# An encoder kernel on one Trainium2 core: the convolution half of the output projection, issued pair by pair of token tiles, and GpSimd's low parts held in program order

## The chip, the core and the metric

One Trainium2 chip, of which the program uses one core. The metric is the device time of one launch in microseconds (us); lower is better. The engines are called PE (matrix products), DVE (vector), ACT (scalar), POOL (GpSimd) and SP (the queue from which the DMAs of this kernel are issued). Each engine works through its own queue in order; semaphores make one wait for another.

## The reference

A prompt and a sample of 512 tokens each, with 16 meta tokens in front, go through one layer in float32. What matters here, cut:

```
z = rms(h) @ w_in                        # -> c_val, c_gate, cq, ckv, k_rope
u = silu(layernorm(conv(c_val * sigmoid(c_gate))))      # 512 channels per token
o = attention(cq, ckv, k_rope)                          # 512 channels per token
h = h + concat([u, o]) @ w_out                          # 1024 x 1024
hf = rms(h)
h = h + (silu(hf @ w_gate) * (hf @ w_up)) @ w_down      # 1024 -> 2816 -> 1024
y = rms(h)
```

## The kernel before

Products are made from pairs: a float32 operand is split into a high part (ACT's cast) and a low part (the rest, a subtraction on DVE or POOL), and `mm3` adds high x high, high x low and low x high, three matmuls for each 128 rows of the contraction.

The 1024 real tokens are eight tiles of 128, `t` = 0 to 7; tile `t` and tile `t + 4` (prompt and sample) form **pair** `t`. The residual rows of tile t are in `hres[t]` (in the rows `h` for 0 to 2, `slots` for 3 to 7).

**Output projection.** `w_out_block(half, dq, t)` adds to quarter `dq` (256 columns) of `hres[t]` the product of one half of the 1024 channels: 12 matmuls of 256 columns into one of four PSUM banks `pt` (L992, the helper's L167 in the rows), then one addition on DVE (L994). Half 1 (attention) comes first, for all tiles. Half 0 (convolution) is 32 blocks, (dq, t); its four weight tiles are `wo[0]`, `wo[2]`, `wo[4]`, `wo[6]`, and they are in the four buffers that the first gate matrix's operands (`wc`) take over, quarter by quarter.

**From a finished tile to the feed-forward's operands.** The feed-forward's products are Strassen products of 2 x 2 blocks (seven products instead of eight; a Winograd form), in which the two token halves (tiles 0 to 3 and 4 to 7) and the two channel halves are the blocks. For each pair t:

- `sq(t)`: once all four quarters of tile t are in, SP stores `hres[t]`, ACT squares and sums it (L192), POOL makes the reciprocal root from it (L193, L194).
- `sc(t)`: DVE scales the tile, two instructions of 512 columns with both tensors in SBUF (L1045).
- `tu(t, s)`: PE transposes tile t (s = 0) or tile t + 4 (s = 1) in 8 matmuls (L1060) into one of two PSUM tiles `px`.
- `do(t, stages)`: the high parts on ACT (L1064, and the copies L1077 and L1080), the sums `t1` to `t4` on DVE (L1086, L1087, L1091, L1094) and the low parts (L1067). Low parts of `a11`, `a12`, `a22` are made by DVE from PSUM; those of the sums `s2`, `s3` (stage x) and `s1`, `s4` (stage y) by POOL, or by DVE where `S_DVE[t]` lists 0, 1 (x) or 2, 3 (y). In the rows `s3` and `a11`, `a22` are called `act`.

**Feed-forward units.** A unit is 256 columns of `w_gate` or `w_up`. `co(j)` (`Unit.comb`) makes the j-th weight operand of unit 0: sums of the loaded blocks on DVE (L1136), the high part on ACT (L1152), the low part on POOL (L1154). `pr(j)` makes product j of unit 0 for the first 256 of a half's 512 token columns, that is for the pairs 0 and 1; the loop over units makes the other 256 columns of unit 0 (pairs 2 and 3) and after each of these products calls `comb(j)` of unit 1. Unit 1's weights are loaded into `hres[2]` and `hres[6]`, which are free once pair 2's low parts are made. From unit 1 on a product has 512 columns.

**What sets the order.** A scheduler orders the instructions of each engine by priorities and a modelled time; those that went through `pin` while `pinned[0]` is set keep the order of the program. It is set from the list of steps on to the end of unit 0. The list is written out by hand:

```
def run(steps):
    for step in steps:
        if isinstance(step, tuple):
            w_out_block(0, *step)
        else:
            step()
```

Of the kernel before, what the change touches and what calls it, by code (L numbers as in the profile page):

```python
# [12 lines left out]
F32 = mybir.dt.float32  # L13
# [71 lines left out]
LO_W = 1024  # L85
ORDER = "Q K S0 S1 T0 T3 M0 T1 M1 S2 T2 M2 T4 M4 M3 S3 E C"
U0_DVE = ()
S_DVE = ((), (), (), (0, 1))


def real_col(s):
# [10 lines left out]
def encoder_kernel(ctx: ExitStack, tc: tile.TileContext, x, meta, gains, w_in, w_kr, small, conv_w, wq, wk, wv,  # L102
# [10 lines left out]
    def name(p):  # L113
        n_tile[0] += 1
        return f"{p}_{n_tile[0]}"
# [9 lines left out]
    def pin(ins):  # L125

        return in_order(ins) if pinned[0] else ins

    def in_order(ins):
        tc.keep_in_program_order(ins)  # L130
        return ins
# [3 lines left out]
    def slot(i):  # L135
        return slots[:, i, :]
# [399 lines left out]
    sq = [slot(0), slot(1)]  # L536
# [451 lines left out]
    def w_out_block(half, dq, t):  # L988
        s, cs, ds = t // 4, slice(t % 4 * 128, t % 4 * 128 + 128), slice(dq * 256, (dq + 1) * 256)
        pt = bank()  # L990
        w = wo[2 * dq + half]
        mm3(pt[:, :256], [(act[half][s][0][:, k, cs], act[half][s][1][:, k, cs]) for k in range(4)],  # L992
            [tuple(wx[:, k * 256:(k + 1) * 256] for wx in w) for k in range(4)])
        pin(nc.vector.tensor_add(hres[t][:, ds], pt[:, :256], hres[t][:, ds]))  # L994
# [27 lines left out]
    a11, a22, s3 = act[0][0], act[1][1], act[0][1]  # L1022
    hf2 = [comb.tile([P, D], F32, name=f"hf{i}") for i in range(2)]
    a12, s1, s2, s4 = (operand(comb, n) for n in ("a12", "s1", "s2", "s4"))


# [9 lines left out]
    def ffn_square(t):  # L1036

        nc.sync.dma_start(h_dram[t * 128:(t + 1) * 128, :], hres[t])
        k4 = hres[t].rearrange("p (k n) -> p k n", k=4)
        ffn_rs[t] = rms_scale(k4, P, s4[1][:, :, 256:512])  # L1040

    def ffn_scale(t):
        for e in range(2):
            h, g = (a[:, e * 512:(e + 1) * 512].rearrange("p (k n) -> p k n", k=4) for a in (hres[t], g_ffn))
            pin(nc.vector.scalar_tensor_tensor(normed_half(t, e), h, ffn_rs[t], g, ALU.mult, ALU.mult))  # L1045

    class Turn:
# [21 lines left out]
        def do(self, stages):  # L1069
            b11, b12 = self.pts[0]  # L1070
            b21, b22 = self.pts[1] if len(self.pts) > 1 else (None, None)
            t1, t2, t3, t4 = self.ts
            own = [nc.vector if i in S_DVE[self.t] else nc.gpsimd for i in range(4)]
            for stage in stages:
                if stage == "a":
                    self.high(a11, b11)
                    pin(nc.scalar.copy(t1, b11))  # L1077
                    self.high(a12, b12)
                elif stage == "A":
                    pin(nc.scalar.copy(t4, b22))  # L1080
                    self.high(a22, b22)
                elif stage == "b":
                    self.low(a11, b11, nc.vector)
                    self.low(a12, b12, nc.vector)
                elif stage == "c":
                    pin(nc.vector.tensor_sub(t3, t1, b21))  # L1086
                    pin(nc.vector.tensor_sub(t1, b22, t3))  # L1087
                    self.high(s2, t1)
                    self.high(s3, t3)
                elif stage == "e":  # L1090
                    pin(nc.vector.tensor_sub(t2, b12, t1))  # L1091
                    self.high(s4, t2)
# [25 lines left out]
    class Unit:  # L1118
# [19 lines left out]
        def comb(self, j):  # L1138
            b11, b12, b21, b22 = (self.block(a, b) for a in range(2) for b in range(2))
            if j == 2:  # L1140
                self.temp("t1", b12, b11)
                self.temp("t2", b22, self.t["t1"])
            if j == 3:
                self.temp("t3", b22, b12)
            if j == 5:
                self.temp("t4", b21, self.t["t2"])
            src = (b11, b21, self.t.get("t2"), self.t.get("t3"), self.t.get("t1"), self.t.get("t4"), b22)[j]
            n = self.u * 7 + j
            if n % 2 == 0:
                two_ops[0] = stream.tile([P, 2, 1024], F32R, tag="pair", bufs=4, name=name("wc"))  # L1150
            w = two_ops[0][:, n % 2, :]
            pin(nc.scalar.copy(w[:, 0:512], src))  # L1152
            lo_eng = nc.vector if self.u in U0_DVE else nc.gpsimd
            lo_eng.tensor_sub(w[:, 512:1024], src, w[:, 0:512].bitcast(F32))  # L1154
# [35 lines left out]
    units = [Unit(u) for u in range(NFF)]  # L1190
# [44 lines left out]
    def w_out_rest(dqs, ts):  # L1235
        for dq in dqs:
            for t in ts:
                w_out_block(0, dq, t)

    w_out_rest(range(3), (0, 4, 1, 5))  # L1240

    pinned[0] = True

# [8 lines that stand above are left out]
    def sq(t):  # L1252
        return lambda: ffn_square(t)

    def sc(t):
        return lambda: ffn_scale(t)

    def co(j):
        return lambda: units[0].comb(j)

    def pr(j):
        return lambda: units[0].product(j, slice(0, 256))
# [3 lines left out]
    def tu(t, s):  # L1266
        def begin():
            if not s:
                turns[t] = Turn(t)
            turns[t].turn(s)  # L1270
        return begin

    def do(t, stages):
        return lambda: turns[t].do(stages)

    units[0].load()
    run([(3, 0), sq(0), (3, 4), sq(4), (3, 1), sq(1), sc(0), (3, 5), sq(5), sc(4), (0, 2), (0, 6),
         tu(0, 0), do(0, "a"), sc(1), (0, 3), tu(0, 1), do(0, "A"), do(0, "b"), (0, 7), do(0, "ce"), sc(5), (1, 2),
         do(0, "xd"), (1, 6), do(0, "y"), (1, 3), co(0), (1, 7),
         tu(1, 0), do(1, "a"), (2, 2), tu(1, 1), do(1, "A"), do(1, "b"), co(1), (2, 6), do(1, "ce"), (3, 2),  # L1280
         do(1, "x"), sq(2), do(1, "d"),
         (3, 6), sq(6), do(1, "y"), co(2), (2, 3), sc(2), (2, 7), sc(6), co(3), co(4), (3, 3), sq(3),
         tu(2, 0), do(2, "a"), tu(2, 1), do(2, "A"), co(5), (3, 7), sq(7)])

    run([pr(0), do(2, "b"), sc(3), co(6), pr(1), do(2, "ce"), pr(2), sc(7), do(2, "x"), pr(3), pr(4),
         tu(3, 0), do(3, "a"), do(2, "dy"), units[1].load, pr(5), do(3, "b"), pr(6), tu(3, 1), do(3, "Ace")])
    left = [[do(3, "x")], [do(3, "dy")]]


    n_pairs = NFF // 2  # L1290
# [3 lines left out]
    def reuse(key):  # L1294
        pool = ops if key.startswith("act") else comb
        return pool.tile([P, 4, SEQ], F32R, tag=key, bufs=1, name=name("re")).rearrange("p a b -> p (a b)")
# [141 lines left out]
    y, junk = (reuse(ld_places[i]).bitcast(F32) for i in (0, 1))  # L1438
# [93 lines left out]
```

## Time and profile before

| | us |
|---|---|
| median of 3 runs | 1107.52 (1107.51 to 1107.55) |
| the profiled execution, its own time | 1107.57 |
| its span, first to last instruction | 1105.8 |
| PE busy in the span | 1081.4 (98%) |
| DVE busy | 824.0 (75%) |
| ACT busy | 498.7 (45%) |
| POOL busy | 477.3 (43%) |

Times in rows are from the span's start; 1.8 us of the profiled execution's time lie around its span. The mean granted clock of PE is 0.992 of full speed. In this program half 0 of the output projection begins at 401.84 us, the products of unit 0 at 458.5, those of unit 1 at 488.43 and those of unit 2 at 508.84. A row of the order in time gives the start, the length, the engine, the line, the operation, what is written and read, and in brackets how long the engine stood idle before it and what released it.

### The profile page before, as it was taken

The page shows a single profiled execution, that of the slowest core. Times are in us where ns is not written, and L with a number is a line of the kernel's source. Part 1 is how long each engine was busy: PE and PEld are TensorE (multiplying, and loading weights), DVE is VectorE, ACT ScalarE, POOL GpSimd, SP SyncE. Part 2 cuts the span into 40 slices and gives each one's busy share as a digit, 9 for nine tenths or more (in the row PEclk, how much of TensorE's full clock was granted, in tenths as well). Part 3 has the DMA queues.
Part 4 walks back from the last instruction along what each step waited for, and adds up shares of the span by engine and source line. Part 5 has one row for each costly group of instructions (what it writes and reads, how often), then busy time and mean ns, then how long its engine had stood idle before and what let it go on. Part 6 is the DMA issues. An engine that isn't in the chain of part 4 may idle for free.

```text
span 1105.8 us, 16021 instructions
## 1 busy us (share of the span) xinstructions
PE 1081.4 (98%) x5922; PEld 935.2 (85%) x5922; DVE 824.0 (75%) x1204; ACT 498.7 (45%) x836; POOL 477.3 (43%) x421
## 2 busy tenths in 40 slices
PE   8999999999999999989999999999999999999997
PEld 8989888888888999878888888888888888888886
DVE  5699997888887546888767776877787595657643
ACT  6554525787786534542333223222323355433331
POOL 4689636563562323865545555554455200000012
PEclk9999999999999999889999999999999999999999
DMA  7211112010111311325264436434542999865503
GB/s 293 78 39 49 39 39 63 37 57 1 39 39 57 116 58 77 127 85 208 94 201 174 145 130 203 159 105 181 190 170 87 306 335 334 284 205 177 181 24 133
DMA packets 71422, 147.08 MB, mean 133 GB/s; under 512 B 6944, under 2 KB 29728, under 8 KB 71344
## 3 DMA queue, kind: packets, MB, share of 16 engines
q1 hardware_dynamic: 71344, 146.06, 38.3%
q8 instruction: 47, 0.77, 0.3%
q14 instruction: 31, 0.25, 0.1%
HBM read 105.92 MB, written 40.11 MB: 132 GB/s over the span
## 4 chain that ended last, share of the span: by engine, by line
PE 83%; DVE 9%; ACT 3%; issue 2%; DMA 2%; POOL 1%; SPq 0%; POOLq 0%; ACTq 0%; DVEq 0%
PE pt L167 59%; PE ps L167 13%; PE pt L797 3%; PE pt L767 2%; PE pt L298 2%; DVE ps L389 2%; DVE ps L397 2%; DVE pacc L399 1%; PE px L277 1%; PE pt L588 1%; ACT p L739 1%; DMA gain<-in_gains_dram 1%; DMA h<-in_w_up_dram 0%; DVE sst L738 0%; DVE kl L156 0%
## 5 line engine op out<-in xcount | busy, mean ns | idle before, releaser
L167 PE MATMUL pt<-act_h,wc 128*128 128x512 f32 (+1 forms) x552 | 177.2, 384 | 0.0
L1154 POOL TENSOR_TENSOR wc<-tt,wc 128x512 fp32r<-128x512 f32 x88 | 123.2, 1416 | 107.8 <-ACT wc L1152 58.4
L167 PEld LDWEIGHTS pt<-act_h,wc 128*128 128x128 f32 x552 | 104.3, 192 | 19.6
L193 POOL TENSOR_SCALAR ms<-ms 128x1 f32<-128x1 f32 x15 | 7.8, 521 | 231.8 <-ACT re L192 213.8
L1152 ACT CAST wc<-tt 128x512 fp32r<-128x512 f32 x88 | 51.6, 619 | 124.5 <-PE pt L167 111.3
L167 PE MATMUL pt<-hn_h,wp 128*128 128x512 f32 (+2 forms) x448 | 107.0, 331 | 0.0
L167 PE MATMUL pt<-act_l,wc 128*128 128x512 f32 (+1 forms) x276 | 105.9, 384 | 0.2 <-DVE act_l L1067 0.2
L1334 DVE TENSOR_TENSOR re<-re,re 128x1024 fp32r<-128x1024 f32 x53 | 64.2, 1224 | 44.8 <-ACT re L1333 43.2
L1333 ACT CAST re<-re 128x1024 fp32r<-128x1024 f32 x53 | 55.3, 1055 | 66.9 <-PE pt L167 22.6
L167 PE MATMUL pt<-re 128*128 128x512 f32 x360 | 84.0, 389 | 0.0
L167 PEld LDWEIGHTS pt<-hn_h,wp 128*128 128x128 f32 x448 | 75.8, 188 | 8.4
L167 PEld LDWEIGHTS pt<-re 128*128 128x128 f32 x360 | 67.6, 188 | 14.0
L152 POOL TENSOR_TENSOR wp<-raw,wp 128x1024 fp32r<-128x1024 f32 x24 | 58.6, 2441 | 40.7 <-ACT wp L149 40.7
L167 PE MATMUL pt<-hn_l,wp 128*128 128x512 f32 (+2 forms) x224 | 74.4, 332 | 0.0
L742 POOL TENSOR_SCALAR p<-p,sst 128x512 f32<-128x512 f32 x64 | 44.2, 696 | 65.0 <-DVE sst L740 57.2
L167 PE MATMUL pt<-wp,act_h 128*128 128x256 f32 x384 | 72.0, 288 | 0.1
L1154 POOL TENSOR_TENSOR wc<-raw,wc 128x512 fp32r<-128x512 f32 x33 | 44.1, 1349 | 52.7 <-ACT wc L1152 52.7
L167 PE MATMUL ps<-re 128*128 128x512 f32 x276 | 63.9, 389 | 0.0
L167 PEld LDWEIGHTS pt<-act_l,wc 128*128 128x128 f32 x276 | 53.0, 192 | 10.1 <-DVE act_l L1067 0.4
L367 POOL TENSOR_TENSOR pacc<-pacc,prod 128x512 f32<-128x512 f32 x43 | 58.3, 1357 | 7.0 <-ACT prod L365 4.3
L167 PEld LDWEIGHTS pt<-wp,act_h 128*128 128x128 f32 x384 | 60.7, 195 | 0.4 <-DVE slots L994 0.4
L167 PEld LDWEIGHTS ps<-re 128*128 128x128 f32 x276 | 51.8, 188 | 10.7
(295 smaller groups left out, 2941.7 us busy)
## 6 DMA issues: line engine op xcount, KB each, us to landing
raw<-in_w_gate_dram SPq DMA_DIRECT2D x22, 512.0 KB, 3.9
hf<-in_w_down_dram SPq DMA_DIRECT2D x44, 256.0 KB, 4.6
re<-in_w_down_dram SPq DMA_DIRECT2D x31, 256.0 KB, 4.6
raw<-in_w_in_dram SPq DMA_DIRECT2D x12, 512.0 KB, 3.6
slots<-in_w_up_dram SPq DMA_DIRECT2D x11, 512.0 KB, 3.5
h<-in_w_up_dram SPq DMA_DIRECT2D x11, 512.0 KB, 5.4
d_t1t<-hf SPq DMA_DIRECT2D x22, 256.0 KB, 5.3
d_t4t<-hf SPq DMA_DIRECT2D x22, 256.0 KB, 2.5
```

The costliest lines, as they stand in the source:

```text
L152: nc.gpsimd.tensor_sub(lo[:, a], raw[:, a], hi[:, a].bitcast(F32))
L167: pin(nc.tensor.matmul(out_ap, lhsT=w_, rhs=m_, start=first and i + j == 0, stop=last and i == n - 1 and j == 2))
L298: in_order(nc.tensor.matmul(pt[:, :n], lhsT=w_[:, k * 128:(k + 1) * 128], rhs=m_[:, k, c0:c0 + n], start=j + k == 0, stop=j == 2 and k == ...
L367: nc.gpsimd.tensor_add(acc, acc, to)
L389: nc.vector.scalar_tensor_tensor(a_, half_win(c, 0, i, HS + 1), k, a_, ALU.mult, ALU.add)
L397: nc.vector.scalar_tensor_tensor(m_, both[:, :, i:i + HS], k, m_, ALU.mult, ALU.add)
L742: nc.gpsimd.tensor_scalar(pr[:, real], pr[:, real], st[:, 2, t:t + 1], 1.0, op0=ALU.mult, op1=ALU.mult)
L797: nc.tensor.matmul(self.po, lhsT=v, rhs=p_, start=self.done + j == 1, stop=self.done + j == 5)
L1152: pin(nc.scalar.copy(w[:, 0:512], src))
L1154: lo_eng.tensor_sub(w[:, 512:1024], src, w[:, 0:512].bitcast(F32))
L1333: nc.scalar.copy(w[:, :, LO], blocks[n])
L1334: nc.vector.tensor_sub(w[:, :, HI], blocks[n], w[:, :, LO].bitcast(F32))
```

## The change

Three edits:

1. The twelve blocks of quarters 0 to 2 for the tiles 0, 4, 1, 5, which stood ahead of the pinned list and were left to the scheduler, are now in the list, and the list goes pair by pair: all quarters of tiles 0 and 4, then of 1 and 5, 2 and 6, 3 and 7, so that the last quarter of pair 2's second tile, block (3, 6), is followed by eight blocks instead of four, and that of its first, (3, 2), by twelve instead of five; the turns of pair 2 stand between the last blocks. All weight operands of unit 0 (`co`) and stage d of pair 2 come before the first product.
2. The low parts of the weight operands on POOL are pinned.
3. All four low parts of the sums of pair 3 are made by DVE, where it was two.

```diff
-S_DVE = ((), (), (), (0, 1))
+S_DVE = ((), (), (), (0, 1, 2, 3))
...
-            lo_eng.tensor_sub(w[:, 512:1024], src, w[:, 0:512].bitcast(F32))
+            pin(lo_eng.tensor_sub(w[:, 512:1024], src, w[:, 0:512].bitcast(F32)))
...
-    w_out_rest(range(3), (0, 4, 1, 5))
...
-    run([(3, 0), sq(0), (3, 4), sq(4), (3, 1), sq(1), sc(0), (3, 5), sq(5), sc(4), (0, 2), (0, 6),
...
-         do(1, "x"), sq(2), do(1, "d"),
-         (3, 6), sq(6), do(1, "y"), co(2), (2, 3), sc(2), (2, 7), sc(6), co(3), co(4), (3, 3), sq(3),
-         tu(2, 0), do(2, "a"), tu(2, 1), do(2, "A"), co(5), (3, 7), sq(7)])
-    run([pr(0), do(2, "b"), sc(3), co(6), pr(1), do(2, "ce"), pr(2), sc(7), do(2, "x"), pr(3), pr(4),
-         tu(3, 0), do(3, "a"), do(2, "dy"), units[1].load, pr(5), do(3, "b"), pr(6), tu(3, 1), do(3, "Ace")])
-    left = [[do(3, "x")], [do(3, "dy")]]
+    run([(0, 0), (1, 0), (2, 0), (0, 4), (1, 4), (2, 4), (3, 0), sq(0), (3, 4), sq(4),
+         (0, 1), (1, 1), sc(0), (2, 1), sc(4), (3, 1), sq(1), tu(0, 0), do(0, "a"), (0, 5), tu(0, 1), do(0, "A"), do(0, "b"),
+         (1, 5), do(0, "ce"), (2, 5), do(0, "d"), (3, 5), sq(5), do(0, "x"),
+         (0, 2), sc(1), (1, 2), sc(5), do(0, "y"), (2, 2), (3, 2), sq(2), tu(1, 0), do(1, "a"), (0, 6), tu(1, 1), do(1, "A"),
+         do(1, "b"), (1, 6), do(1, "ce"), (2, 6), do(1, "d"), (3, 6), sq(6),
+         (0, 3), sc(2), do(1, "x"), (0, 7), sc(6), co(0), do(1, "y"), (1, 3), tu(2, 0), do(2, "a"), co(1), (1, 7),
+         tu(2, 1), do(2, "A"), do(2, "b"), co(2), (2, 3), co(3), do(2, "ce"), (2, 7), do(2, "d"), co(4), (3, 3), sq(3),
+         co(5), (3, 7), sq(7), co(6)])
+    run([pr(0), sc(3), pr(1), sc(7), pr(2), do(2, "xy"), units[1].load, pr(3), tu(3, 0), do(3, "a"), pr(4), do(3, "b"),
+         tu(3, 1), do(3, "A"), pr(5), do(3, "ce"), pr(6), do(3, "x")])
+    left = [[do(3, "dy")]]
```

Outside of this part the queues of all five engines hold the same instructions in the same order as before; SP's queue is the same throughout.

DVE's queue where pair 2 is scaled (`hf` are the scaled tiles 2 and 6, L994 the additions of blocks, `tt` the sums of unit 0's weight blocks). Before: pt_5286 is block (3, 6), pt_5315 and pt_5331 are (2, 3) and (2, 7), pt_5354 is (3, 3), pt_5401 is (3, 7), the last of the 32.

```order
L994 TENSOR_TENSOR slots<-pt_5286,slots 128x256
L1136 TENSOR_TENSOR tt_5308<-raw_4953,raw_4951 128x512
L1136 TENSOR_TENSOR tt_5310<-raw_4953,tt_5308 128x512
L994 TENSOR_TENSOR slots<-pt_5315,slots 128x256
L1045 SCALAR_TENSOR_TENSOR hf_4773<-h_4132,rs_5279,gain_4133 128x512 x2
L994 TENSOR_TENSOR slots<-pt_5331,slots 128x256
L1045 SCALAR_TENSOR_TENSOR hf_4774<-slots,rs_5302,gain_4133 128x512 x2
L1136 TENSOR_TENSOR tt_5347<-raw_4953 128x512
L994 TENSOR_TENSOR slots<-pt_5354,slots 128x256
L1136 TENSOR_TENSOR tt_5397<-raw_4951,tt_5310 128x512
L994 TENSOR_TENSOR slots<-pt_5401,slots 128x256
```

Now: pt_5223 is (3, 6), pt_5243 and pt_5261 are (0, 3) and (0, 7), pt_5282 and pt_5310 are (1, 3) and (1, 7), px_5296 is the turn of tile 2.

```order
L994 TENSOR_TENSOR slots<-pt_5223,slots 128x256
L994 TENSOR_TENSOR slots<-pt_5243,slots 128x256
L1045 SCALAR_TENSOR_TENSOR hf_4773<-h_4132,rs_5143,gain_4133 128x512 x2
L994 TENSOR_TENSOR slots<-pt_5261,slots 128x256
L1045 SCALAR_TENSOR_TENSOR hf_4774<-slots,rs_5239,gain_4133 128x512 x2
L994 TENSOR_TENSOR slots<-pt_5282,slots 128x256
L994 TENSOR_TENSOR slots<-pt_5310,slots 128x256
L1067 TENSOR_TENSOR act_l<-px_5296,act_h 128x4x128
L1067 TENSOR_TENSOR a12l<-px_5296,a12h 128x4x128
L1136 TENSOR_TENSOR tt_5337<-raw_4785,raw_4783 128x512
L1136 TENSOR_TENSOR tt_5339<-raw_4785,tt_5337 128x512
```

The scaling of pair 2 comes with seven and six blocks still to be added, where it was three and two, and unit 0's weight sums now stand behind it.

POOL's queue at the end of the list (`wc` are weight operands' low parts: wc_5441 before and wc_5432 now hold co(6) of unit 0 and co(0) of unit 1; the `h_4132` and `slots` of the first four L1067 are pair 2). Before:

```order
L1154 TENSOR_TENSOR wc_5441<-raw_4953,wc_5441 128x512
L1067 TENSOR_TENSOR s2l<-h_4132,s2h 128x4x128
L1067 TENSOR_TENSOR act_l<-slots,act_h 128x4x128
L1067 TENSOR_TENSOR s1l<-slots,s1h 128x4x128
L1067 TENSOR_TENSOR s4l<-h_4132,s4h 128x4x128
L1154 TENSOR_TENSOR wc_5441<-h_4132,wc_5441 128x512
L1067 TENSOR_TENSOR s1l<-slots,s1h 128x4x128
L1067 TENSOR_TENSOR s4l<-slots,s4h 128x4x128
L1154 TENSOR_TENSOR wc_5627<-h_4132,wc_5627 128x512
```

Now:

```order
L1154 TENSOR_TENSOR wc_5432<-raw_4785,wc_5432 128x512
L1067 TENSOR_TENSOR s2l<-h_4132,s2h 128x4x128
L1067 TENSOR_TENSOR act_l<-slots,act_h 128x4x128
L1067 TENSOR_TENSOR s1l<-slots,s1h 128x4x128
L1067 TENSOR_TENSOR s4l<-h_4132,s4h 128x4x128
L1154 TENSOR_TENSOR wc_5432<-h_4132,wc_5432 128x512
L1154 TENSOR_TENSOR wc_5627<-h_4132,wc_5627 128x512
```

The two low parts of pair 3, which stood behind unit 1's first operand, have left POOL. They are now in DVE's queue, behind pair 3's other low parts (px_5536 is the turn of tile 7, pt_5568 the last product of unit 0's first half, pt_5612 the second of its other half):

```order
L1183 TENSOR_TENSOR h_4130<-pt_5568,slots 128x256
L1067 TENSOR_TENSOR s2l<-slots,s2h 128x4x128
L1067 TENSOR_TENSOR act_l<-slots,act_h 128x4x128
L1094 TENSOR_TENSOR slots<-slots,px_5536 128x512
L1067 TENSOR_TENSOR act_l<-px_5536,act_h 128x4x128
L1067 TENSOR_TENSOR s1l<-slots,s1h 128x4x128
L1067 TENSOR_TENSOR s4l<-slots,s4h 128x4x128
L1183 TENSOR_TENSOR h_4130<-pt_5612,h_4131 128x256
```

Before, the rows of s1l and s4l were not in this queue, and the addition of a product of the second half stood between those of s3 (here `act_l<-slots`) and t4 (L1094).

More of the change, by code (lines that the diff above doesn't have):

```diff
@@ L1276, in encoder_kernel @@
     units[0].load()
-    run([(3, 0), sq(0), (3, 4), sq(4), (3, 1), sq(1), sc(0), (3, 5), sq(5), sc(4), (0, 2), (0, 6),
-         tu(0, 0), do(0, "a"), sc(1), (0, 3), tu(0, 1), do(0, "A"), do(0, "b"), (0, 7), do(0, "ce"), sc(5), (1, 2),
-         do(0, "xd"), (1, 6), do(0, "y"), (1, 3), co(0), (1, 7),
-         tu(1, 0), do(1, "a"), (2, 2), tu(1, 1), do(1, "A"), do(1, "b"), co(1), (2, 6), do(1, "ce"), (3, 2),
-         do(1, "x"), sq(2), do(1, "d"),
-         (3, 6), sq(6), do(1, "y"), co(2), (2, 3), sc(2), (2, 7), sc(6), co(3), co(4), (3, 3), sq(3),
-         tu(2, 0), do(2, "a"), tu(2, 1), do(2, "A"), co(5), (3, 7), sq(7)])
-    run([pr(0), do(2, "b"), sc(3), co(6), pr(1), do(2, "ce"), pr(2), sc(7), do(2, "x"), pr(3), pr(4),
-         tu(3, 0), do(3, "a"), do(2, "dy"), units[1].load, pr(5), do(3, "b"), pr(6), tu(3, 1), do(3, "Ace")])
-    left = [[do(3, "x")], [do(3, "dy")]]
+    run([(0, 0), (1, 0), (2, 0), (0, 4), (1, 4), (2, 4), (3, 0), sq(0), (3, 4), sq(4),
[9 more added lines that the diff above has]
+    left = [[do(3, "dy")]]
     n_pairs = NFF // 2
```

## The prediction

> **What bounds the kernel now.** I read the page's busy shares and slices first, then what PE waited for, then PE's order in time where it waited.
>
> ```profile
> span 1105.8 us, 16021 instructions
> PE 1081.4 (98%) x5922; PEld 935.2 (85%) x5922; DVE 824.0 (75%) x1204; ACT 498.7 (45%) x836; POOL 477.3 (43%) x421
> PE   8999999999999999989999999999999999999997
> PEclk9999999999999999889999999999999999999999
> ```
>
> PE is the bound nearly everywhere. One slice is 27.6 us, and only the 17th and 18th, 442 to 498, show a lower clock: the end of the output projection and the first unit, which the change rewrites. Behind them there is nothing to be had or lost: this window (PE busy, then PEld, DVE, ACT, POOL, clock, DMA) has PE busy in 590.24 of 591 us.
>
> ```profile
> 509.00:1100.00 591.00, 590.24 (x2604) 488.55 (x2603) 414.98 (x512) 201.31 (x292) 194.78 (x149) 1.00 0.54 184
> ```
>
> So each microsecond that PE gains before 509 should reach the end. What PE waited for from 397 to 520, and the granted clock in four windows (7th column):
>
> ```profile
> PE px L1060 <- DVE hf L1045: 2.6, 3, 1.6
> PE pt L167 <- POOL s1l L1067: 1.8, 1, 1.8
> PE px L1060 <- DVE act_l L1067: 1.8, 1, 1.8
> PE pt L167 <- DVE s2l L1067: 0.4, 1, 0.4
> PE pt L167 <- DVE act_l L1067: 0.2, 1, 0.2
> ...
> 191.00:195.00 4.00, 3.27 (x19) 2.58 (x20) 2.25 (x6) 2.40 (x7) 4.00 (x6) 1.00 0.50 133
> ...
> 453.00:460.00 7.00, 6.06 (x28) 5.69 (x29) 5.01 (x6) 3.32 (x7) 5.69 (x4) 0.52 0.32 96
> 473.00:477.20 4.20, 4.05 (x21) 3.85 (x20) 2.72 (x5) 2.03 (x5) 2.52 (x2) 0.59 0.31 103
> 484.00:487.40 3.40, 3.40 (x16) 3.40 (x17) 2.83 (x5) 1.24 (x2) 3.40 (x3) 0.51 0.00 0
> ```
>
> There are three stalls, 6.8 us in all. Each of the three longest (1.6, 1.8, 1.8) is followed by some 3.4 us or more at half clock: 3.4 us of work at 0.51 is 1.7 us lost, so a stall of 1.8 costs about 3.5. The first window is for a wait of 1.40 us (the row with the bracket, below), and the clock stayed at 1.00.
>
> ```profile
> 191.26 0.39 PE L167 MATMUL ps<-kh,ql 128*128 128x264 f32 x1 [1.40 <-ACT p L739]
> ...
> 401.84 0.40 PE L167 MATMUL pt<-wp,act_h 128*128 128x256 f32 x2
> 427.76 1.04 PE L1060 MATMUL px<-ident,hf 128*128 128x128 f32 x8
> 428.55 0.48 PE L167 MATMUL pt<-wp,act_h 128*128 128x256 f32 x2
> 440.42 1.04 PE L1060 MATMUL px<-ident,tt 128*128 128x128 f32 x8
> 449.80 0.28 PE L167 MATMUL pt<-wp,act_l 128*128 128x256 f32 x1
> 460.62 0.28 PE L167 MATMUL pt<-a12h,wc 128*128 128x256 f32 x1
> 462.06 0.28 PE L167 MATMUL pt<-s2h,wc 128*128 128x256 f32 x1
> 463.50 0.28 PE L167 MATMUL pt<-act_h,wc 128*128 128x256 f32 x1
> 470.19 0.28 PE L167 MATMUL pt<-s4h,wc 128*128 128x256 f32 x1
> 480.25 0.28 PE L167 MATMUL pt<-act_h,wc 128*128 128x256 f32 x1
> 492.52 0.39 PE L167 MATMUL pt<-a12h,wc 128*128 128x512 f32 x1
> 508.84 0.39 PE L167 MATMUL pt<-act_h,wc 128*128 128x512 f32 x1
> ```
>
> Undisturbed prices: 12 matmuls of 256 columns 1.44 (462.06 to 463.50), a turn 0.79 (427.76 to 428.55), a product of unit 1 2.72 (six of them from 492.52 to 508.84, where unit 2 begins). The PE work from block (0, 0) at 401.84 to unit 2 is 32 blocks, 8 turns, 14 half products, 7 whole ones: 46.08 + 6.32 + 20.16 + 19.04 = 91.6, an end at 493.44. It ended at 508.84: **15.4 us are lost.** Each stretch less its work: 449.92 to 460.62 (two turns, a block, a product: 4.46) loses 6.2; 470.31 to 480.25 (a turn, three products: 5.11) 4.8; 480.25 to 492.52 (four products and unit 1's first: 8.48) 3.8; 0.5 is scattered.
>
> **What the change does to each stall.** The rows behind them:
>
> ```profile
> 446.24 0.69 DVE L1067 TENSOR_TENSOR act_l<-px,act_h 128x512 fp32r<-128x512 f32 x1
> 446.83 0.42 DVE L994 TENSOR_TENSOR slots<-pt,slots 128x256 f32<-128x256 f32 x1
> 447.17 1.34 DVE L1136 TENSOR_TENSOR tt<-raw,raw 128x512 f32<-128x512 f32 x1
> 449.69 1.41 DVE L1045 SCALAR_TENSOR_TENSOR hf<-h,rs,gain 128x512 f32<-128x512 f32 x2
> 451.55 3.42 DVE L1045 SCALAR_TENSOR_TENSOR hf<-slots,rs,gain 128x512 f32<-128x512 f32 x2
> 478.02 0.69 DVE L1067 TENSOR_TENSOR s2l<-slots,s2h 128x512 fp32r<-128x512 f32 x1
> ...
> 421.28 1.06 ACT L192 ACTIVATE s4l<-h 128x1024 fp32r<-128x1024 f32 x1 [17.92 <-DVE h L994]
> 480.26 0.62 ACT L1152 CAST wc<-h 128x512 fp32r<-128x512 f32 x1 [0.96 <-DMA h<-in_w_up_dram]
> ...
> 422.83 0.56 POOL L194 TENSOR_TENSOR rs<-ms,tiny 128x1 f32<-128x1 f32 x1
> 480.96 1.30 POOL L1154 TENSOR_TENSOR wc<-h,wc 128x512 fp32r<-128x512 f32 x1 [5.03 <-ACT wc L1152]
> 482.22 1.71 POOL L1067 TENSOR_TENSOR s1l<-slots,s1h 128x512 fp32r<-128x512 f32 x1
> ...
> 475.96 0.33 SPq L1128 DMA_DIRECT2D h<-in_w_up_dram  x1
> ```
>
> A scaling pair (L1045) takes 1.41 on a quiet DVE and 3.42 while POOL makes low parts: 0.7 or 1.7 for one instruction. A block's addition costs DVE 0.34 (446.83 to 447.17). From a square's start to the reciprocal root it is 2.1 (421.28 to 422.83 + 0.56). From the start of a pair's second turn (440.42) to the end of its last DVE low part before stage x (446.24 + 0.69) it is 6.5.
>
> *First stall, scaling pair 2.* In the new order PE reaches pair 2's second turn after 28 blocks and 5 turns, at 401.84 + 40.32 + 3.95 = 446.1. Pair 1's second turn starts at 401.84 + 21 x 1.44 + 3 x 0.79 = 434.4, its DVE chain ends at 440.9, block (3, 6) is added at 441.3, the root is there at 443.4, tile 6 is scaled by 444.9 (quiet) or 446.9 (POOL then has pair 1's s2 and s3). Its second half is needed at 446.5: a wait of 0 to 0.4; I take 0.2. Before, this scaling came three blocks from the end; now five blocks lie behind the first turn.
>
> *Where the lateness goes: scaling pair 3.* DVE now has pair 2's chain and unit 0's sums t1 to t3 (L1136; 0.7 to 1.7 each, the one above 1.34) ahead of block (3, 3). From 446.3: 6.5, three sums at 1.1, 0.34, the root 2.1, behind one POOL low part 1.3, and a first half scaled beside POOL, 1.7: 461.5. PE has 32 blocks, 6 turns and 4 products until it needs this, 401.84 + 46.08 + 4.74 + 5.76 = 458.4. So it waits 3.1 in all, 2.9 more. With sums at 0.7, no idle in the chain and a quiet POOL it is none; with sums at 1.7 and the chain slower by as much it is 4.8. I take 2.9, since POOL's queue is full there. A part of it will appear earlier, as waits for a PSUM bank that DVE has not emptied.
>
> *Second stall, tile 7's turn.* The other scaling of pair 3 follows at 462.2 plus an addition, 1.41 to 3.42 long: 464 to 466. PE, 3.1 late, needs the first half at 463.8 and the second 0.4 later: 0 to 1.8; I take 0.6. Before, stages c to d of pair 2 (DVE) stood ahead of it; now they are done ahead of the products.
>
> *Third stall, s1's low part.* POOL made it behind unit 1's first operand, which waited for a load: issued at 475.96, when pair 2's last low part had freed the tile, ready at 480.26, 4.3 later; POOL stood idle for 5.03, and s1l began at 482.22. Now DVE makes s1l and s4l, 0.6 to 0.7 each since POOL has nothing then (as in the row at 478.02). From the second scaling's end at 465: five additions of products and two more, seven at 0.34, three sums and the low parts of a11, a12, s2, s3, t4, a22, s1 at 0.6: 2.4 + 6 = 8.4, so 473.4. The product that needs it comes at 464.32 (32 blocks, 8 turns, 7 products) + 5.88 + 3.7 = 473.9. No wait, with 0.5 in hand; at the worst 2.0. The Trainium skill, in SBUF — State Buffer, section Who interferes with whom, says that a DVE instruction with two SBUF inputs and a GpSimd instruction that reads SBUF block one another for a whole instruction. The 3.42 against 1.41 above agrees. By this rule the two moved low parts would cost 2 more if POOL were at work beside them.
>
> *Unit 1's load.* It follows POOL's four low parts of pair 2, which now come right behind co(6): about 464 + 4 x 1.3 to 1.7 = 470. Landed 4.3 later, plus cast and low part (0.62 + 1.30): 476.5. Unit 1 begins at 474.4 + 3.7 = 478.1 or later. Hidden, by 1.6.
>
> *At no cost:* the twelve blocks moved into the list are the same matmuls; their weights are ready (PE runs blocks without a gap there), and the additions fit a DVE that is idle between them until then. Pinning POOL's low parts costs what the order above shows, counted already.
>
> **The sum.** Waits 0.2 + 2.9 + 0.6 = 3.7. One of them will be over 1.5 and halve the clock once: 1.7 by the windows. Scattered, as before, 0.5. Loss 5.9 instead of 15.4, a gain of 9.5. The profiled execution took 1107.57 (0.05 over the median): 1098.0 against the median. The ends: no loss at all, 1092.2; all upper ends, 0.4 + 4.8 + 1.8 + 2.0 with three halved clocks (5.1) and 0.5, a loss of 14.6, 1106.7. The Trainium skill, in TensorE: Matmul & The Clock Gate, part 1 on the HAM clock gate, has the clock halved after at least one idle window of about 3.4 us. In this trace 1.6 to 1.8 us sufficed, and 1.40 did not. By its rule the clock term would be 0 and the time 1096.3.
>
> **Rivals.**
> 1. *DVE becomes the bound.* It is nearly without idle from 442 to 474. There are 16 instructions with two SBUF inputs in that stretch (8 scalings, 4 sums, 4 low parts), each 1.0 dearer beside POOL; I have counted about half so. The others add up to 8, on PE's path since nothing else waits: 1102 to 1106.7. For it: POOL's queue has some fifteen low parts in the same time. Against: POOL is empty for the last 4 us.
> 2. *No clock loss, shorter waits.* The wait for pair 3 is split into pieces of 1.40 or less, as the PSUM banks would do: 1.7 less, 1096.3, and down to 1092.2 where DVE is quicker.
> 3. *Slower: unit 1's load late.* If pair 2's low parts or SP's queue hold it, ACT stands at co(0) with all that is queued behind it. It must be late by 1.6 + 9.5 + 2.2 = 13.3 us, landing at 488, before the kernel is slower by 0.2%. Before it landed at 480 with PE later, and SP's order is the same.
>
> **How the numbers follow.** My case, 1096.5 to 1101.5, 0.50; rival 2 0.24; rival 1 0.18, of which 0.06 ends within 0.2% (2.2 us, about what a measurement can tell); rival 3 0.06; some other wait that eats all of it, no change, 0.02. Faster 0.50 + 0.24 + 0.12 = 0.86, same 0.08, slower 0.06. From 1093.8 to 1103.0 there lie my case, nearly all of rival 2 and a third of rival 1, about 0.8.
>
> **What would show it.** PE dense from 401.84 to about 446; a wait at pair 2's second turn under 1 us; the longest wait at pair 3's first turn or the banks before it, released by L1045 or L994; none on s1l; unit 1 from 478; unit 2 from about 499 (493.44 + 5.9); behind that the same rows, 9 to 10 us earlier. Wrong if DVE shows 1.7 for most two-input rows from 442 to 474, or the clock is halved twice.

## The result, and the profile after

The changed kernel takes **1099.63 us** (median, 1099.49 to 1100.09) against 1107.51 (1106.02 to 1107.79) for the kernel before, run beside it: 7.9 us less, ratio 0.9932 with a 95% interval of 0.9921 to 0.9942. The forecast was 1098.0, from 1093.8 to 1103.0. The profiled execution took 1100.08; its span is 1098.3. Ratios here and below are not the quotient of the two medians.

From the page of after: span, busy shares, and PE and its granted clock in 40 slices.

```profile
span 1098.3 us, 16027 instructions
PE 1075.8 (98%) x5922; PEld 929.5 (85%) x5922; DVE 829.0 (75%) x1206; ACT 497.5 (45%) x836; POOL 475.9 (43%) x419
PE   8999999999999999899999999999999999999997
PEclk9999999999999999999999999999999999999999
```

No slice shows a lower clock any more. Between the first slice and the last, only the 17th, from 439 to 467, is below nine tenths. What PE waited for from 397 to 520 (total, times, longest):

```profile
PE px L1060 <- DVE tt L1045: 2.6, 3, 1.4
PE px L1060 <- DVE hf L1045: 1.5, 2, 1.0
PE pt L167 <- ACT act_h L1064: 1.0, 1, 1.0
```

It was 6.8 us in seven waits, it is 5.1 in six; none is over 1.40, and none is on `s1l`. By stretch (PE's busy time is the first figure behind the length, the clock is the column ahead of the last two):

```profile
404.00:446.00 42.00, 41.97 (x353) 41.61 (x352) 27.38 (x51) 17.15 (x32) 13.41 (x18) 1.00 0.23 89
446.00:454.00 8.00, 6.51 (x54) 6.10 (x54) 7.96 (x9) 3.02 (x7) 8.00 (x6) 1.00 0.01 2
454.00:470.00 16.00, 12.43 (x99) 11.46 (x98) 13.89 (x21) 9.17 (x18) 13.84 (x13) 1.00 0.46 147
470.00:520.00 50.00, 50.00 (x269) 43.47 (x269) 48.67 (x63) 18.73 (x37) 32.61 (x21) 1.00 0.49 158
```

Between 446 and 454 DVE and POOL are both busy for all of 8 us while PE is not: that is where to look. PE's order in time, each row with a wait, and the first row of unit 1:

```profile
447.60 0.63 PE L1060 MATMUL px<-ident,hf 128*128 128x128 f32 x4 [0.54 <-DVE hf L1045]
449.18 0.65 PE L1060 MATMUL px<-ident,hf 128*128 128x128 f32 x4 [0.95 <-DVE hf L1045]
458.00 0.36 PE L167 MATMUL pt<-a12h,wc 128*128 128x256 f32 x1 [0.98 <-ACT act_h L1064]
464.02 1.23 PE L1060 MATMUL px<-ident,tt 128*128 128x128 f32 x8 [1.40 <-DVE tt L1045]
466.92 0.63 PE L1060 MATMUL px<-ident,tt 128*128 128x128 f32 x4 [0.24 <-DVE tt L1045]
468.50 0.66 PE L1060 MATMUL px<-ident,tt 128*128 128x128 f32 x4 [0.95 <-DVE tt L1045]
...
481.95 0.40 PE L167 MATMUL pt<-act_h,wc 128*128 128x512 f32 x1
```

The wait at 458.00 is put down to a cast that was long done; the DVE addition that emptied the product's PSUM bank (block (2, 7), four uses of a bank earlier) ended at 457.84. At the prediction's prices (32 blocks, 8 turns, 14 half products) unit 1 could begin at 401.88 + 72.56 = 474.4. It begins at 481.95: **7.5 us are lost where it was 15.4**, and the difference, 7.9, is the gain.

### The profile page after: what moved, and what is told of

It is laid out like the page before. It is cut to its first block, busy times and chain, and to the rows that moved or that the text cites. A ratio compares the mean times of both kernels' runs of the same rounds, so it can differ in the third digit from the quotient of the medians.

```text
span 1098.3 us, 16027 instructions
## 1 busy us (share of the span) xinstructions
PE 1075.8 (98%) x5922; PEld 929.5 (85%) x5922; DVE 829.0 (75%) x1206; ACT 497.5 (45%) x836; POOL 475.9 (43%) x419
## 4 chain that ended last, share of the span: by engine, by line
PE 56%; DVE 2%; issue 2%; DMA 0%; POOL 0%; ACT 0%; POOLq 0%; ACTq 0%; SPq 0%; DVEq 0%
PE pt L167 48%; PE ps L167 8%; DMA raw<-in_w_gate_dram 0%; DVE tt L1045 0%; DVE hf L1045 0%; DVE tt L1136 0%; DVE slots L994 0%; DVE act_l L1067 0%; POOL rs L194 0%; DVE h L1087 0%; POOL slots L1442 0%; DVE slots L1086 0%; DVE slots L1094 0%; DVE a12l L1067 0%; DVE h L1091 0%
```

## Experiments

The theory after the result: the three stalls of before and the half clock behind them went, as forecast; what is left, and more than forecast, is DVE's chain of scalings, sums and additions from 428 to 470, stretched by POOL's reads of SBUF beside it and by queues in order. Rivals: edit 3 made the gain; the pin does nothing; what is left is POOL's queue alone, or DVE's own length.

Times of different chips are compared through the kernel before, which ran beside each (1107.0 to 1107.5). Since a wait early in the program sometimes costs 0.9 us (last section), the profiles are compared by **D**, the time from the first row of tile 0's turn to the first row of unit 1: 62.8 us in after (419.16 to 481.95). At the prediction's prices alone it would be 55.3 (72.56 less the 12 blocks ahead of the turn). D is left out where PE takes unit 1's first matmuls among the last ones of unit 0, and for the old list.

| kernel | us | ratio to before, 95% | D |
|---|---|---|---|
| after, again | 1100.03 | 0.9934 (0.9921 to 0.9948) | 62.8 |
| S1, S4 low parts on POOL | 1101.62 | 0.9935 (0.9921 to 0.9949) | |
| without the pin | 1105.78 | 0.9979 (0.9969 to 0.9989) | 68.3 |
| list alone | 1105.82 | 0.9980 (0.9971 to 0.9989) | |
| before with edit 3 | 1105.66 | 0.9974 (0.9963 to 0.9985) | |
| low parts moved | 1096.86 | 0.9905 (0.9892 to 0.9919) | 59.6 |
| the same, block 5 later | 1095.89 | 0.9898 (0.9884 to 0.9911) | 58.9 |
| two more moves | 1096.56 | 0.9898 (0.9880 to 0.9915) | 58.6 |
| pair 0's low parts moved | 1098.05 | 0.9914 (0.9899 to 0.9928) | 61.2 |
| all low parts of pairs on DVE | 1101.01 | 0.9940 (0.9925 to 0.9955) | 63.4 |
| low parts as memsets | 1092.79 | 0.9869 (0.9856 to 0.9883) | 55.8 |
| memsets, three times each | 1095.63 | 0.9892 (0.9876 to 0.9909) | 58.1 |

### The three edits apart

**Edit 3 undone.**

```diff
-S_DVE = ((), (), (), (0, 1, 2, 3))
+S_DVE = ((), (), (), (0, 1))
```

> The kernel after with S_DVE[3] back at (0, 1): the low parts of the fourth pair's S1 and S4 go to POOL again. Theory (the gain came from the list; the two low parts lie beside products 5 and 6 on either engine): POOL is idle from 472.1 to 478.25 in the trace after, DVE's 476.38 start of S1's low part shows when its inputs are there, so POOL does them at about 476.4 to 479.0, and the weight low part of unit 1 that stands at 478.25 starts some 0.8 us later, with product 6 running until 481.95: 1099.6, within 0.3 us either way. Rival (the move of the low parts to DVE is what removed the third stall of before, 3.8 us): S1's low part on POOL at 1.3 us instead of 0.69 makes unit 2 wait, 1101 to 1103.4.

1101.62, where after takes 1099.63 and 1100.03: up to 2 us more, but after did not run on that chip, and the ratios don't tell the kernels apart; the spans of the profiles differ by 0.9 (1099.2 and 1098.3). No wait on `s1l` is back, so the rival's mechanism is refuted, but "within 0.3" missed too. A row of PE and one of DVE in this kernel, and DVE's in after:

```profile
510.26 0.47 PE L167 MATMUL pt<-act_h,wc 128*128 128x512 f32 x1 [0.54 <-DVE slots L1187]
...
507.83 1.69 DVE L1199 TENSOR_TENSOR slots<-slots 128x512 f32<-128x512 f32 x1
```

```profile
507.15 0.69 DVE L1199 TENSOR_TENSOR slots<-slots 128x512 f32<-128x512 f32 x1
```

POOL begins unit 1's weights 1.2 us later (479.49 for 478.25). At 507 it is still 0.3 late and DVE 0.7, and now one of its low parts (507.68) runs beside the DVE sum at 507.83, which takes 1.69 instead of 0.69; the addition behind it is late and PE waits 0.54 in unit 2. The three products up to there take 8.97 (501.29 to 510.26) where they took 8.16 in after (501.02 to 509.18), 0.8 of the 0.9 between the profiles; for the rest of the 2 us no run shows a cause. The edit pays in another place than the prediction thought, and little.

**The pin undone.**

```diff
-            pin(lo_eng.tensor_sub(w[:, 512:1024], src, w[:, 0:512].bitcast(F32)))
+            lo_eng.tensor_sub(w[:, 512:1024], src, w[:, 0:512].bitcast(F32))
```

> The kernel after without the pin on POOL's weight low parts; only the order on POOL's queue and on one stretch of SP's changes: the root (pow) for tile 7's square stands behind the low part of weight block 6 and the four low parts of the third pair. Theory (every stall left is a queue in order that delays a scaling): from 464.05, where the root starts in the trace after, five low parts of about 1.3 us come first, so the root ends at about 471.1 and not at 464.97; tile 7's scaling then takes 1.41 alone instead of 3.45 beside POOL, and ends at about 472.5 instead of 468.45. PE waits about 4 us more ahead of tile 7's turn and works at half clock for some us behind it (1.7 us): 1103.7 to 1105.5. Rival (the pin only fixes an order that was so anyway, or the late root hides behind products 2 and 3, which PE does first): 1099.6 within 0.5.

1105.78, a little above the theory's range: of the change's 7.9 us, 6 are gone. The rows of POOL, DVE and PE, and PE's clock behind the wait:

```profile
466.63 1.29 POOL L1067 TENSOR_TENSOR s2l<-h,s2h 128x512 fp32r<-128x512 f32 x1
...
471.54 0.56 POOL L194 TENSOR_TENSOR rs<-ms,tiny 128x1 f32<-128x1 f32 x1
472.14 1.41 DVE L1045 SCALAR_TENSOR_TENSOR tt<-slots,rs,gain 128x512 f32<-128x512 f32 x2 [6.27 <-POOL rs L194]
473.03 1.94 PE L1060 MATMUL px<-ident,tt 128*128 128x128 f32 x8 [5.36 <-DVE tt L1045]
...
470.00:482.00 12.00, 8.97 (x62) 9.00 (x63) 8.79 (x17) 4.23 (x10) 2.10 (x3) 0.73 0.51 164
```

An unpinned low part let the scheduler put five low parts ahead of a root of 0.56 us. DVE then stood idle for 6.27 with pair 3's chain behind it, PE for 5.36, and the clock fell (0.73 as the mean from 470 to 482). In the kernel before, the same pin alone moves no instruction on any of the five queues: what it is worth comes only with the new list.

**The list alone** (edits 2 and 3 undone).

> The new list alone: after without the pin and with S_DVE[3] at (0, 1). Theory: as the kernel without the pin, 1103.7 to 1105.5, and up to 1 us more because the fourth pair's S1 and S4 low parts stand on POOL behind work that is now late; so the list alone gives 2 to 4 us of the 7.9 and the pin the rest. Rival (list alone carries all of the gain): 1099.6 within 0.5.

1105.82: as without the pin, and 1.7 us under before, less than the 2 to 4 expected. Its waits are those of the kernel without the pin, the 5.4 included.

**Edit 3 alone, on the kernel before.**

```diff
-S_DVE = ((), (), (), (0, 1))
+S_DVE = ((), (), (), (0, 1, 2, 3))
```

> The kernel before with S_DVE[3] = (0, 1, 2, 3) alone. Theory: it touches only the third stall of before (3.8 us ahead of the fourth pair's S1 product, with its half clock); the first two stalls stay (6.2 and 4.8 us). The low part no longer stands on POOL, but the cast of S1's high part stays late in ACT's queue, so most but not all of the stall goes: 1107.5 less about 3, 1104 to 1105.5. Rival (the low parts on DVE delay sums and gate work of unit 0, or the cast alone sets the stall): 1107.5 within 0.5.

1105.66, 1.8 less than before and just above the theory's range. Three of PE's waits:

```profile
PE px L1060 <- DVE act_l L1067: 1.5, 1, 1.5
PE pt L167 <- ACT s2h L1064: 1.4, 1, 1.4
PE pt L167 <- DVE s1l L1067: 0.8, 1, 0.8
```

The wait on S1 falls from 1.8 on POOL to 0.8 on DVE; a wait of 1.4 on the cast of S2 is new. So list and edit 3 give some 1.7 and 1.8 each alone, 1.7 together without the pin, and 7.9 with it; list and pin without edit 3 give 5.9 by the medians. The edits don't add.

### Where the rest is lost

**Control.** The kernel after on another chip.

> The kernel after, unchanged, for the chip that runs the next three. Both theories: 1099.6 within 1 us. If it comes out near 1101.6, as the kernel with S1 and S4 on POOL did on the chip before, that kernel's 2 us are the chip and not the edit.

1100.03, with the same waits.

**POOL's low parts at other places of the list** (nothing added or left out; S2 and S3 ahead of the next square, S1 and S4 behind it):

```diff
-         (1, 5), do(0, "ce"), (2, 5), do(0, "d"), (3, 5), sq(5), do(0, "x"),
-         (0, 2), sc(1), (1, 2), sc(5), do(0, "y"), (2, 2), (3, 2), sq(2), tu(1, 0), do(1, "a"), (0, 6), tu(1, 1), do(1, "A"),
-         do(1, "b"), (1, 6), do(1, "ce"), (2, 6), do(1, "d"), (3, 6), sq(6),
-         (0, 3), sc(2), do(1, "x"), (0, 7), sc(6), co(0), do(1, "y"), (1, 3), tu(2, 0), do(2, "a"), co(1), (1, 7),
+         (1, 5), do(0, "ce"), (2, 5), do(0, "d"), do(0, "x"), (3, 5), sq(5),
+         (0, 2), sc(1), (1, 2), sc(5), (2, 2), (3, 2), sq(2), do(0, "y"), tu(1, 0), do(1, "a"), (0, 6), tu(1, 1), do(1, "A"),
+         do(1, "b"), (1, 6), do(1, "ce"), (2, 6), do(1, "d"), do(1, "x"), (3, 6), sq(6),
+         (0, 3), sc(2), (0, 7), sc(6), (1, 3), co(0), do(1, "y"), tu(2, 0), do(2, "a"), co(1), (1, 7),
```

> The kernel after with POOL's low parts at other places of the list: those of a pair's S2 and S3 (do x) ahead of the square that the next scaling hangs on, those of S1 and S4 (do y) behind the next square, for pairs 0 and 1, and weight block 0's preparation behind block (1, 3). Nothing is added or left out. Theory (the stalls left come from scalings that run beside POOL's low parts at 1.7 instead of 0.7 for one instruction, and POOL's queue in order): the scaling of tile 5 takes 1.41 and not 3.46, the chain of pair 1 ends 2 to 3 us sooner, the first stall (2.0) goes, and the later ones shrink: 1096 to 1097.5. Rival (the additions and sums set the end, the scalings' length hides): 1099.6 within 0.5. Second rival (low parts that come later hold up the products): 1100 to 1102.

1096.86, as the theory had it: 3.2 us under the control. The first stall shrinks to a wait of 0.6 but does not quite go, since tile 6's scaling still takes 3.46; the wait of 1.0 at the bank goes.

**The first two of these lines alone, for pair 0** (and `do(0, "y")` behind `sq(2)`, as above).

> The kernel after with POOL's low parts of pair 0 alone moved (do x ahead of block (3, 5) and its square, do y behind tile 2's square); pairs 1 to 3 and the weights as in after. Theory (the first stall, 2.0 us at pair 2's second turn, begins with tile 5's scaling at 430.9, which runs beside pair 0's low parts at 3.46): that scaling takes about 1.42, tile 2's square starts some 2 us earlier, pair 1's casts on ACT behind it too, tile 6's scaling (still beside pair 1's low parts, 3.45) starts 1 to 1.5 us earlier, and the first stall shrinks from 2.0 to about 0.6; the later ones keep most of their size: 1098 to 1099. Rival (pair 1's own low parts beside tile 6's scaling make the stall): the stall stays, 1099.6 to 1100.5.

1098.05, and the first stall is a wait of 0.4 instead of 1.5. The chain in the kernel after, rows of POOL, DVE and ACT:

```profile
430.82 1.30 POOL L1067 TENSOR_TENSOR s2l<-h,s2h 128x512 fp32r<-128x512 f32 x1
...
430.89 3.46 DVE L1045 SCALAR_TENSOR_TENSOR tt<-slots,rs,gain 128x512 f32<-128x512 f32 x2 [0.43 <-POOL rs L194]
435.10 1.06 ACT L192 ACTIVATE s4l<-h 128x1024 fp32r<-128x1024 f32 x1 [5.38 <-issue]
437.73 0.69 DVE L1067 TENSOR_TENSOR act_l<-px,act_h 128x512 fp32r<-128x512 f32 x1 [2.38 <-ACT a12h L1064]
```

And with pair 0's low parts moved:

```profile
430.88 1.41 DVE L1045 SCALAR_TENSOR_TENSOR tt<-slots,rs,gain 128x512 f32<-128x512 f32 x2 [0.43 <-POOL rs L194]
433.04 1.06 ACT L192 ACTIVATE s4l<-h 128x1024 fp32r<-128x1024 f32 x1 [3.59 <-issue]
435.67 0.69 DVE L1067 TENSOR_TENSOR act_l<-px,act_h 128x512 fp32r<-128x512 f32 x1 [0.60 <-ACT a12h L1064]
```

Tile 5's scaling starts at the same time in both. Beside POOL's low parts it takes 3.46, without them 1.41; the additions behind it, tile 2's square, pair 1's casts behind that square on ACT, and pair 1's low parts on DVE are then all 2.1 us earlier. The later waits keep their sizes (0.97 at the bank, 1.41 at pair 3): this scaling made the first stall and not those.

**Low parts as memsets.** In the helper, and likewise for the weights' low parts:

```diff
+            if eng is nc.gpsimd:
+                return pin(eng.memset(op[1][:, :, self.cs].bitcast(F32), 0.0))
```

> The kernel after with each of POOL's low parts from the list on (the four low parts of pairs 0 to 2, and the weights' low parts of the first units' preparation) replaced by a memset of the same tile: the same bytes are written, none is read, and the low parts are left zero, so part of the computation is left out. Theory (port contention with POOL's reads stretches DVE's two-input instructions; some 9.4 us of excess between 430 and 477 in the trace after): scaling pairs take 1.41 everywhere, sums 0.7, the loss of 7.5 before unit 2 falls to 1 to 3, and the time to 1093 to 1096. Rival (in-order queues alone: the waits for ACT's casts and squares and POOL's roots stay, as long as they are): 1098 to 1099.6, with scalings at 1.41 but PE's waits where they are. Second rival (POOL's writes lock DVE out as well): scalings stay at 3.4, 1099.6 within 1.

1092.79: faster by 7.2 than the control, just under the theory's range, and PE waits for nothing from 397 to 520. The scalings of the tiles 5, 3, 7 (`tt`) and 6 (`hf`), with minimum, median and maximum in ns, in after and then in this kernel:

```profile
L1045 DVE SCALAR_TENSOR_TENSOR tt<-slots,rs,gain x6: 739/1758/1778, 430.9 to 466.7; 128x512 f32<-128x512 f32 x6
L1045 DVE SCALAR_TENSOR_TENSOR hf<-slots,rs,gain x2: 1750/1762/1774, 445.7 to 447.4; 128x512 f32<-128x512 f32 x2
```

```profile
L1045 DVE SCALAR_TENSOR_TENSOR tt<-slots,rs,gain x6: 746/750/752, 431.8 to 460.3; 128x512 f32<-128x512 f32 x6
L1045 DVE SCALAR_TENSOR_TENSOR hf<-slots,rs,gain x2: 743/746/750, 445.0 to 445.6; 128x512 f32<-128x512 f32 x2
```

The memsets run beside the scalings too and cost them nothing. The Trainium skill, in SBUF — State Buffer, section Who interferes with whom, says that a DVE instruction with two SBUF inputs contends with a GpSimd instruction that reads SBUF, not with one that only writes it; these rows agree (0.75 beside a memset, up to 1.78 beside a subtraction). But a memset is also shorter (0.53 for 1.3), so this run alone doesn't part the reads from the length of POOL's queue.

**The memsets three times over**, which takes POOL 1.64 us for each low part.

```diff
-                return pin(eng.memset(op[1][:, :, self.cs].bitcast(F32), 0.0))
+                for _ in range(3):
+                    pin(eng.memset(op[1][:, :, self.cs].bitcast(F32), 0.0))
+                return
```

> The kernel with the low parts as memsets, each memset written three times over, so that POOL is occupied for about 1.4 us by each, a little longer than by the subtraction (1.3), and still reads nothing; the low parts are left zero, so part of the computation is left out. It parts the two things that the single memset changed at once: POOL's reads of SBUF and the time that POOL's queue is taken. Theory (the reads stretch DVE's two-input instructions, and that is the loss): scalings stay at 0.75 each, and there is next to no PE wait before unit 2, 1092.4 to 1094. Rival (POOL's queue being short made the difference, as roots came sooner): scalings at 0.75 but the roots late, PE's waits back to 2 to 5 us, 1095 to 1099.

1095.63, in the rival's range by its time, between the two by its one wait. The scalings stay at 0.75 or less, so what stretches them is POOL's reads and not that POOL is at work. Every wait of after but the one at tile 3's turn is gone. Tile 3's scaling waits for the root behind POOL's memsets, 4.29 where it was 1.82 in after (PE, DVE, POOL):

```profile
461.21 1.23 PE L1060 MATMUL px<-ident,tt 128*128 128x128 f32 x8 [1.57 <-DVE tt L1045]
460.31 1.42 DVE L1045 SCALAR_TENSOR_TENSOR tt<-slots,rs,gain 128x512 f32<-128x512 f32 x2 [4.29 <-POOL rs L194]
452.72 6.59 POOL L1160 MEMSET wc<- 128x512 f32 x12
459.71 0.57 POOL L194 TENSOR_TENSOR rs<-ms,tiny 128x1 f32<-128x1 f32 x1
```

D falls from 62.8 to 58.1 with POOL's queue no shorter than in after (from 425 to 475 it is busy for 36.9 us, in after 32.9), and to 55.8 with a short one: of the 7.0 us, some 4.7 go with the reads, and 2.3 with POOL's time, mostly ahead of tile 3's root. Both theories hold a part; the reads hold the larger. The split is rough: a memset also waits for no cast, for which POOL stood idle up to 1.83 us in after, and no run parts that from the reads.

**All four low parts of every pair on DVE.**

```diff
-S_DVE = ((), (), (), (0, 1, 2, 3))
+S_DVE = ((0, 1, 2, 3),) * 4
```

> The kernel after with the four low parts of every pair on DVE (S_DVE holds 0 to 3 for all four), so that POOL keeps only the weights' low parts and the roots. Twelve more DVE instructions of 0.68 between 424 and 475, 8.2 us. Theory (DVE's queue is what PE waits for, whatever fills it): DVE gains back the scalings of tiles 5 and 6 (2 us each) and part of tile 7's, but has 8.2 us more in the same time, so the waits grow by 1 to 4 us and a half clock may come with one: 1100.5 to 1105. Rival (POOL beside DVE is all that costs): 1096 to 1098.

1101.01, 1 us slower than the control. Nine of the twelve scaling instructions of the tiles 1, 5, 2, 6, 3 and 7 are at 0.75 or under (five in after), but the twelve more instructions use that up, and waits on DVE appear behind them (two of them in the rows; PE waits 5.0 in all):

```profile
PE pt L167 <- DVE act_l L1067: 0.7, 1, 0.7
PE pt L167 <- DVE s2l L1067: 0.6, 1, 0.6
```

### A better order

**Low parts moved, and weight block 5 behind the last square.**

```diff
-         co(5), (3, 7), sq(7), co(6)])
+         (3, 7), sq(7), co(5), co(6)])
```

> The kernel with the moved low parts, and weight block 5's preparation behind the last square too, so that no weight low part stands on POOL between tile 3's and tile 7's squares. Theory (POOL's root for the last scalings stands behind low parts, and the last scaling runs beside one): the third pair's stalls shrink by another 0.5 to 1 us against the kernel with the moved low parts alone: 1095 to 1097. Rival (ACT then casts block 5 too late for product 5, or DVE is the bound there): the same as that kernel within 0.3, or 0.5 to 1 slower.

1095.89, the fastest kernel with all of the computation: 4.1 under after on the same chip, 11.6 under before. Against the kernel with the moved low parts alone it is 1.0 faster, with intervals that overlap.

**Two more moves**: block 0 and pair 1's S1 and S4 behind `do(2, "a")`, block 4 behind block (2, 7).

```diff
-         (0, 3), sc(2), (0, 7), sc(6), (1, 3), co(0), do(1, "y"), tu(2, 0), do(2, "a"), co(1), (1, 7),
-         tu(2, 1), do(2, "A"), do(2, "b"), co(2), (2, 3), co(3), do(2, "ce"), (2, 7), do(2, "d"), co(4), (3, 3), sq(3),
+         (0, 3), sc(2), (0, 7), sc(6), (1, 3), tu(2, 0), do(2, "a"), co(0), do(1, "y"), co(1), (1, 7),
+         tu(2, 1), do(2, "A"), do(2, "b"), co(2), (2, 3), co(3), do(2, "ce"), (2, 7), co(4), do(2, "d"), (3, 3), sq(3),
```

> The list with moved low parts and block 5 behind the last square, and two more moves: weight block 0 and do y of pair 1 behind pair 2's first casts (do a), so that ACT holds POOL back while tile 6 is scaled; weight block 4 behind block (2, 7), so that its low part is done before tile 3's square. Theory: tile 6's scaling takes about 1.4 and not 3.45, PE's wait of 0.6 at pair 2's second turn goes, tile 3's root comes 0.5 to 0.9 earlier, the waits at pair 3's turns (1.5 in all) shrink to about 1: 1094 to 1095.5. Rival (what is left is unit 1's load and the low parts behind it, or PE is bound already by the order of its own work): 1095.9 within 0.4.

1096.56: no better. What was to go did go, and came back elsewhere. DVE's rows, and two of PE's three groups of waits:

```profile
445.00 1.41 DVE L1045 SCALAR_TENSOR_TENSOR hf<-slots,rs,gain 128x512 f32<-128x512 f32 x2 [0.43 <-POOL rs L194]
450.09 1.67 DVE L1136 TENSOR_TENSOR tt<-raw,tt 128x512 f32<-128x512 f32 x1
452.02 1.45 DVE L1136 TENSOR_TENSOR tt<-raw 128x512 f32<-128x512 f32 x1
```

```profile
PE pt L167 <- DVE slots L1187: 0.6, 1, 0.6
PE pt L167 <- ACT act_h L1064: 0.5, 1, 0.5
```

Tile 6's scaling is at 1.41 as expected, but the low parts that stood beside it now stand beside the sums of the weights, which took 0.7 in the kernel with block 5 later and take 1.67 and 1.45 here. PE's wait of 0.6 at pair 2 has become 0.5 at a bank and 0.1 more in unit 2.

## Why the prediction was near, point by point

The loss was forecast at 5.9 and is 7.5, each part below by stretch (waits and the slower start behind them):

| term | forecast | measured |
|---|---|---|
| first stall, pair 2's second turn | 0.2 (0 to 0.4) | 2.0 |
| bank and pair 3's first turn | 2.9 (0 to 4.8) | 1.3 + 1.8 = 3.1 |
| tile 7's turn | 0.6 (0 to 1.8) | 1.7 |
| third stall, `s1l` | 0 | 0 |
| half clock | 1.7 | 0 |
| scattered | 0.5 | 0.7 |

- *Right:* the stalls of before and their half clock are what the change removes; PE is dense until 446; the lateness moves to pair 3 and shows first at a bank; unit 1's load is hidden. The sign set for being wrong did not come: of the 16 two-input instructions on DVE that the prediction counted, six took 1.66 to 1.78, two 1.16 and 1.45, eight 0.75 or less.
- *The step that failed* is the first stall's "its DVE chain ends at 440.9". It ended at 442.9. The 6.5 from a turn's start to the last low part were taken from pair 1 of before, where its casts on ACT stood ahead of tile 2's square. In after they stand behind that square, which waits for additions that stand on DVE behind a scaling at 3.46. The rows of before, then of after (where the square starts at 435.10, above):

```profile
440.36 0.60 ACT L1064 CAST a12h<-px 128x512 fp32r<-128x512 f32 x1
446.27 1.06 ACT L192 ACTIVATE s4l<-h 128x1024 fp32r<-128x1024 f32 x1
```

```profile
437.10 0.60 ACT L1064 CAST a12h<-px 128x512 fp32r<-128x512 f32 x1
442.24 0.68 DVE L1067 TENSOR_TENSOR act_l<-px,act_h 128x512 fp32r<-128x512 f32 x1
```

The prediction priced that scaling's length for tile 6 and not for tile 5, two links ahead. Moving pair 0's low parts alone showed it.

- *Pair 3's first turn* agrees by luck as much as by the sum. Tile 3's scaling, 461.5 less 1.7 in the sum, so from 459.8, began at 462.12, 2.3 later; PE had by then lost 2.7 on the way (2.0 and 0.7), and the two shifts nearly cancel.
- *Tile 7's turn* was mis-sized by the same cost: its scaling took 3.45, the upper end of the 1.41 to 3.42 that the prediction allowed. The scalings of tiles 3 and 7 in after:

```profile
462.12 2.42 DVE L1045 SCALAR_TENSOR_TENSOR tt<-slots,rs,gain 128x512 f32<-128x512 f32 x2 [1.82 <-POOL rs L194]
465.00 3.45 DVE L1045 SCALAR_TENSOR_TENSOR tt<-slots,rs,gain 128x512 f32<-128x512 f32 x2
```

- *The half clock* didn't come; the longest wait was 1.40. That is 1.7 less, against 1.8 and 1.1 more from the first and the last turn and 0.4 from the rest: the forecast of 1098.0 is 1.6 low, and by luck closer than its terms.
- *Rival 1* (DVE as the bound by contention) named the right mechanism for what is left, with a price that was too high: 4.7 us of 7.5 by the memsets, roughly. *Rival 2* had its condition met, waits of 1.40 or less and no half clock, but not its time (1096.3 or less), since the waits and slow starts came to 7.5 in all. *Rival 3* didn't occur.
- *The pin* was put at no cost and given no worth of its own. That it carries 6 us under this list was not foreseen; the order after, from which the sum was made, already contained it.

## What to carry to other kernels

Before pricing a step by a duration from the trace, look at which of its instructions read two operands from SBUF on DVE, and what POOL reads at that time in the new order: one such pair cost 2.05 us here, and by way of two queues in order it cost PE 1.6 us some 17 us later. Place POOL's reads beside DVE work that reads from PSUM (an addition of a block takes 0.41 with and without a low part beside it in after), and a short instruction that others wait for, such as a root, ahead of them and held there. Take edits apart singly and together: here two edits gave 1.7 and 1.8 us alone, the third alone moves no instruction, and all three gave 7.9.

## What the hardware showed that was not expected

The length of a wait alone did not decide whether the clock fell. The wait of 1.40 us at 191 is in every kernel of this study, in code that none of them changes, and the prediction took it as showing that 1.40 is safe. In the kernel without the pin the same wait was followed by half clock; the window behind it, in after first, then with the wait in that kernel:

```profile
193.00:195.00 2.00, 1.78 (x12) 1.33 (x11) 0.75 (x4) 1.39 (x3) 2.00 (x4) 1.00 0.63 229
```

```profile
191.37 0.39 PE L167 MATMUL ps<-kh,ql 128*128 128x264 f32 x1 [1.40 <-ACT p L739]
...
193.00:195.00 2.00, 2.00 (x8) 1.45 (x7) 0.46 (x4) 1.39 (x3) 2.00 (x5) 0.55 0.60 246
```

It was halved there in five of fourteen profiles (waits of 1.40 to 1.42) and not in nine (1.39 to 1.41). Tile 0's turn, in the kernels with the new list, then starts at 419.8 to 420.2 instead of 418.9 to 419.3: 0.9 us. The six runs of after lie within 0.6 of each other, the six of before beside them within 1.8; how much of that is this wait, no run shows. Waits of 1.51 (edit 3 alone) and 1.57 (the threefold memsets) left the clock at 1.00; those of 1.63 and more were each followed by half clock. The Trainium skill, in TensorE: Matmul & The Clock Gate, part 1 on the HAM clock gate, says that the activity window of about 3.4 us is free-running; a wait that falls differently in such a window would explain it, but no run here tested that.
